# A hybrid decoder step on one core: splitting the weights with two DMAs and a negated copy, instead of a cast and a subtraction

## The chip, the core and the metric

The kernel runs on one of the eight cores of a Trainium2 chip. A core has TensorE (PE, matrix products; PEld are its weight loads), VectorE (DVE), ScalarE (ACT), GpSimd (POOL) and SyncE (SP), each with its own in-order queue of instructions, an on-chip memory (SBUF) of 128 partitions, PSUM for the results of products, and 16 DMA engines that move data between HBM and SBUF. DMAs are issued by an engine's queue: in this kernel by SP and by POOL. The metric is the device time of one execution in microseconds, median of several runs; less is better.

## The reference

One inference step of one layer: 16 meta tokens and 512 prompt tokens in one group, 8 sample tokens in another, with shared weights. Cut to what matters here:

```python
def branch_inputs(x, pos, norm_gain, w_in, q_norm_gain, k_norm_gain):
    xn = rmsnorm(x, norm_gain)
    h = jnp.einsum('btd,de->bte', xn, w_in)                  # 2048 -> 8704
    q, k, v, z_a, u, z_s, g_a, g_s = jnp.split(h, IN_SPLITS, axis=-1)
    ...

def s5_branch(u, h0, ..., w_glu, b_glu):                     # diagonal state space
    ...
    y = jax.nn.gelu(y.reshape(b, t, SSM_WIDTH))
    y = y * jax.nn.sigmoid(y @ w_glu + b_glu)                # 1024 -> 1024
    return y, h[:, -1]

def merge(x, o_attn, z_a, y_ssm, z_s, g_a, g_s, w_attn_out, w_ssm_out, w_out):
    br_a = (o_attn * jax.nn.silu(z_a)) @ w_attn_out          # 1024 -> 2048
    br_s = (y_ssm * jax.nn.silu(z_s)) @ w_ssm_out            # 1024 -> 2048
    return x + (jax.nn.sigmoid(g_a) * br_a + jax.nn.sigmoid(g_s) * br_s) @ w_out   # 2048 -> 2048
```

Between them stand attention in a sliding window of 128 keys with the meta tokens as sinks, and, for the sample tokens, attention over a cache. Everything is float32.

## The kernel before

**Products.** TensorE works in a shorter float type, float32r. To come near float32, each operand is held as two float32r parts: hi, the operand rounded, and lo, the operand minus hi, rounded. A product is the sum of three: hi*hi, hi*lo and lo*hi. Tokens are the columns: 536 of them in two halves of 268, of which most products use 260. x is kept in SBUF as xh and xl from the start to the end of the first big product.

**The weight stream.** All weights lie in one array of 208 units, each [128, 8, 128] float32 (512 KB), in the order in which they are used. The class `Stream` hands them out: `get` makes units until it is `ahead` units (2) in front of the one in use. A unit is made by `tiles` (buffers raw, whi, wlo, three of each) and `piece`: SP issues the load of raw, ACT casts it to whi, DVE subtracts whi from raw into wlo. These are recorded at high priority. `mm` (the line L843 is its matmul) takes a unit and does 8 k-tiles x 3 products x 2 halves = 48 matmuls of 260 columns into a PSUM pair; there are two such pairs. The first six units are made in pieces, between the loads of x (tiles xr, ten buffers, the name that also keeps early results; their squares are xsq), while x is split into xh and xl.

**Side work.** After each unit `mm` lets `Background.step` record side work with a budget of DVE time per unit: first the state space (`ssm_prep`, then for each of 8 blocks `ssm_consts` and `ssm_block`), then attention (`Attn`: keys, values, queries, blocks of scores, softmax, turn, weigh) and, in a second lane, the sample tokens' attention over the cache (`Attn.sample`). `bg.after` holds the side work of the attention stage behind the last subtraction of the stream.

**Stages.** Up to about 60 us: loads of x, the first units, the norm. To about 640 us: the input products beside the state space. To about 1020 us: the rest of them, the gate of the state-space branch (w_glu) and part of w_ssm_out, beside attention. From there on the last products alone. The results of an input block are scaled on DVE into z (two buffers), get their tanh on ACT, and SP stores them to HBM (gD), from where they come back later.

**Order.** A scheduler sets each engine's order at build time from the recorded work and its priorities; at run time an engine works its queue in that order, and a waiting instruction holds up those behind it. POOL's queue holds before the change: MEMSETs of the state space's tiles U, d and H (lines L333, L312, L340), the loads of the sample's work (L630 to L679), the copies of the windows, and the loads zr (L1094). SP's queue holds everything else that a DMA does, the weights (L781) among it.

Of the kernel before, what the change touches and what calls it, by code (L numbers as in the profile page):

```python
# [14 lines left out]
P = 128  # L15
# [37 lines left out]
def cmul(nc, pool, out, a, br, bi, sh, tag):  # L53
    """out = a * (br + i bi); axis 1 of a and out holds (re, im); sh: the shape behind it."""
# [12 lines left out]
def ssm_prep(nc, cst, tmp, psum, dram, R, ident, a_prm, a_h0):  # L67
    """Constants of the state space: everything [128 = (group of the pair, state), 32 pairs]."""
# [16 lines left out]
    # sin and cos: th minus multiples of pi, half-odd ones for cos  # L85
# [34 lines left out]
    # F = (lam_bar - 1) / lam  # L120
# [13 lines left out]
    # rows of Fk: F1re, Fre, F1im, Fim with F1 = lam_bar * F  # L134
# [15 lines left out]
    # lam_bar ** 2 = r2 * z  # L150
# [16 lines left out]
    def powers(tab, z, cnt, tag):  # L167
        """tab[j] = z ** j, j < cnt; returns z ** 1, 2, 4, 8."""
# [29 lines left out]
    # carry: r2 * z ** 132  # L198
# [7 lines left out]
    # lam_bar * h0, imaginary part negated  # L206
# [17 lines left out]
def ssm_consts(nc, pool, psum, R, D, ub, a_bT, a_bN, a_cT, bdm):  # L224
    """What block ub of 4 pairs needs beside u: stationaries, rotation tables, decay."""
    v = nc.vector
    ps = slice(4 * ub, 4 * ub + 4)
    # stationary of bu: rows (hi|lo copies of (even, odd) x 32 inputs), columns 128 states
# [22 lines left out]
    # C, C * lam_bar, and C * B_bar  # L251
    bN = pool.tile([P, 4, 2, 32], F32, name="bN")
# [27 lines left out]
    kh = pool.tile([P, P], F32R, name="kh")  # L280
    kl = pool.tile([P, P], F32R, name="kl")
# [5 lines left out]
    # rotation tables cos and -sin of (angle of lam_bar ** 2) * j, j < 132  # L287
# [93 lines left out]
    # states out (imaginary parts are held negated)  # L381
# [26 lines left out]
def rsqrt_dve(nc, pool, out, v_, shape, tag, end="t", iters=3):  # L408
    """out = v ** -0.5 by Newton steps from the exponent's half."""
# [11 lines left out]
class Attn:  # L421
# [12 lines left out]
    def load(self, i, W, row):  # L434
        """Block i of the raw k and q rows [128 = (2 heads, 64), 2, W], its halves swapped, and its norms."""
# [16 lines left out]
    def rope(self, parts, W, g, gs):  # L452
        """The loaded rows, normed and turned."""
# [69 lines left out]
    def scores(self, kv, b):  # L523
        """Scores of 128 queries of the 4 heads of kv: 16 meta keys, and 128 of the window."""
# [98 lines left out]
    def sample(self, a_sink, a_kc, a_vc):  # L623
# [33 lines left out]
        for b in range(8):  # L657
            nc.gpsimd.dma_start(out=qD[:, b], in_=qt[8 * b:8 * b + 8])
# [666 lines left out]
```

## Time and profile before

| | us |
|---|---|
| median of 3 runs | 1363.43 (1362.49 to 1364.37) |
| span of the profiled execution | 1363.1 |
| TensorE busy | 1349.8 |
| DVE busy | 913.0 |
| ACT busy | 405.7 |
| POOL busy | 51.8 |
| span in slices: TensorE | over 90% in all slices but two |

The profile gives one execution. The span runs from its first to its last instruction. A row of a group of instructions names the line of the kernel, the engine, the operation, the tile written and those read, the count, then busy time and the mean of one in ns, then the idle time of the engine before them and what ended most of it. An arrow "<-" in a row of waits stands between who waited and whom it waited for. In stage tables each engine has busy time and, in brackets, its number of instructions.

### The profile page before, as it was taken

Reading aid. Unit: us, or ns where it says so; the run is one execution under the profiler, and the core shown is the slowest. Engines: PE = TensorE matmul, PEld = TensorE weight load, DVE = VectorE, ACT = ScalarE, POOL = GpSimd, SP = SyncE. Lnnn points to the kernel's source line nnn. Section 1 sums busy time; section 2 is a strip of 40 time slices with the busy share of each in tenths; the row PEclk is TensorE's granted clock in tenths of the full one; section 3 lists DMA queues with packets and bytes.
Section 4 is the critical chain, followed back from the end, with each engine's and each line's share of the span. In section 5 each row is a group of like instructions: output and inputs, shape, how many; then the busy total and the mean of one; then the engine's idle time right before and its main releaser. Section 6 shows DMA issues by size and latency. Waiting matters only on the chain.

```text
span 1363.1 us, 26678 instructions
## 1 busy us (share of the span) xinstructions
PE 1349.8 (99%) x10996; PEld 1287.3 (94%) x10996; DVE 913.0 (67%) x1779; ACT 405.7 (30%) x686; POOL 51.8 (4%) x122
## 2 busy tenths in 40 slices
PE   9999999999999999999979999999999999999998
PEld 8999999999998989999979999999999999999998
DVE  8887778777968687868477688687876355422221
ACT  7323221222222222222244433335423122211110
POOL 0000000000000000000400211000010000000000
PEclk9999999999999999999999999999999999999999
DMA  8436253535353435343784346336666444444441
GB/s 264 140 116 216 94 173 111 172 94 172 107 160 106 157 105 160 94 134 110 188 234 128 107 151 200 125 120 215 190 208 200 139 140 140 141 137 140 135 136 45
DMA packets 91497, 201.18 MB, mean 148 GB/s; under 512 B 16060, under 2 KB 34732, under 8 KB 91344
## 3 DMA queue, kind: packets, MB, share of 16 engines
q1 hardware_dynamic: 86704, 185.59, 43.4%
q0 software_dynamic: 4672, 13.89, 3.8%
q8 instruction: 86, 1.41, 0.4%
q14 instruction: 35, 0.29, 0.1%
HBM read 171.06 MB, written 30.48 MB: 148 GB/s over the span
## 4 chain that ended last, share of the span: by engine, by line
PE 94%; DMA 3%; SPq 1%; DVE 1%; ACT 1%; issue 0%; DVEq 0%; ACTq 0%
PE mm L843 82%; PE aux L589 2%; PE aux L346 1%; DMA sw<-rawD 1%; PE aux L345 1%; DMA xr<-in_x 1%; PE mm L1188 1%; PE mm L930 1%; PE aux L396 1%; PE aux L534 1%; PE aux L389 1%; PE aux L535 1%; PE aux L1007 1%; PE mm L1125 1%; PE aux L570 1%; DMA rb<-rqD 0%
## 5 line engine op out<-in xcount | busy, mean ns | idle before, releaser
L782 ACT CAST whi<-raw 128x1024 fp32r<-128x1024 f32 (+3 forms) x220 | 219.9, 1004 | 713.9 <-PE mm L843 557.6
L843 PE MATMUL mm<-xh,whi 128*128 128x260 f32 (+1 forms) x2048 | 423.9, 287 | 0.0
L843 PE MATMUL mm<-xl,whi 128*128 128x260 f32 (+1 forms) x2048 | 416.3, 284 | 0.0
L843 PE MATMUL mm<-xh,wlo 128*128 128x260 f32 (+1 forms) x2048 | 416.0, 284 | 0.0
L783 DVE TENSOR_TENSOR wlo<-raw,whi 128x1024 fp32r<-128x1024 f32 (+3 forms) x220 | 255.0, 1163 | 116.2 <-ACT whi L782 112.1
L843 PEld LDWEIGHTS mm<-xh,whi 128*128 128x128 f32 x2048 | 317.5, 189 | 13.1 <-issue 8.5
L843 PEld LDWEIGHTS mm<-xl,whi 128*128 128x128 f32 x2048 | 318.3, 189 | 5.2 <-issue 5.2
L843 PEld LDWEIGHTS mm<-xh,wlo 128*128 128x128 f32 x2048 | 315.3, 188 | 2.8 <-issue 2.8
L843 PE MATMUL mm<-Y,whi 128*128 128x260 f32 x768 | 125.5, 284 | 0.0
L843 PEld LDWEIGHTS mm<-Y,whi 128*128 128x128 f32 x768 | 105.7, 188 | 2.3 <-issue 2.3
L843 PE MATMUL mm<-ml,whi 128*128 128x260 f32 x480 | 96.8, 283 | 0.0
L843 PE MATMUL mm<-mh,whi 128*128 128x260 f32 x480 | 96.4, 282 | 0.0
L843 PE MATMUL mm<-mh,wlo 128*128 128x260 f32 x480 | 96.4, 282 | 0.0
L843 PE MATMUL mm<-A,whi 128*128 128x260 f32 x512 | 82.2, 282 | 0.0
L843 PE MATMUL mm<-Y,wlo 128*128 128x260 f32 x384 | 77.6, 283 | 0.0
L843 PEld LDWEIGHTS mm<-mh,whi 128*128 128x128 f32 x480 | 73.9, 189 | 0.0
L843 PEld LDWEIGHTS mm<-ml,whi 128*128 128x128 f32 x480 | 73.8, 188 | 0.0
L843 PEld LDWEIGHTS mm<-mh,wlo 128*128 128x128 f32 x480 | 73.8, 188 | 0.0
L843 PEld LDWEIGHTS mm<-A,whi 128*128 128x128 f32 x512 | 70.2, 188 | 0.0
L870 DVE TENSOR_TENSOR z<-mm,R 128x520 f32<-128x520 f32 x43 | 30.0, 697 | 49.9 <-PE mm L843 48.6
L843 PEld LDWEIGHTS mm<-Y,wlo 128*128 128x128 f32 x384 | 59.2, 188 | 0.4 <-issue 0.4
L843 PE MATMUL mm<-A,wlo 128*128 128x260 f32 x256 | 51.6, 283 | 0.0
(371 smaller groups left out, 1467.2 us busy)
## 6 DMA issues: line engine op xcount, KB each, us to landing
raw<-in_w SPq DMA_DIRECT2D x202, 512.0 KB, 3.9
gD<-z SPq DMA_DIRECT2D x48, 260.0 KB, 2.2
t<-gD SPq DMA_DIRECT2D x32, 260.0 KB, 2.7
cache<-in_kc POOLq DMA_DIRECT2D x15, 288.0 KB, 3.5
cache<-in_vc POOLq DMA_DIRECT2D x15, 288.0 KB, 3.4
xr<-in_x SPq DMA_DIRECT2D x16, 268.0 KB, 6.3
t<-in_x SPq DMA_DIRECT2D x16, 260.0 KB, 3.5
f<-FD SPq DMA_DIRECT2D x64, 64.0 KB, 2.4
```

Source lines behind the costliest of these rows:

```text
L345: nc.tensor.matmul(bu[:, i, 0:272], lhsT=D["bh"][:, i, a], rhs=U[:, a], start=True, stop=False)
L346: nc.tensor.matmul(bu[:, i, 0:272], lhsT=D["bl"][:, i, a], rhs=U[0:64, a], start=False, stop=True)
L389: nc.tensor.matmul(y[32 * a:32 * a + 32, 0, 0:NE], lhsT=D["cl"][:, a, i], rhs=H[:, a, i, 0:NE], start=(i == 0), stop=False, skip_group_che ...
L396: nc.tensor.matmul(y[32 * a:32 * a + 32, 1, 0:272], lhsT=D["c"][:, a, i], rhs=H[:, a, i, 1:273], start=(i == 0), stop=(i == 1))
L534: nc.tensor.matmul(ps[:, e, 0:272], lhsT=q, rhs=KH[:, k0:k0 + 272], start=True, stop=False)
L535: nc.tensor.matmul(ps[:, e, 0:272], lhsT=q, rhs=KL[:, k0:k0 + 272], start=False, stop=True)
L570: nc.tensor.transpose(out=ps[:, 0, 128 * r:128 * r + 128], in_=Pn[:, r], identity=C["idn"])
L589: nc.tensor.matmul(pv[64 * e:64 * e + 64, 0, 0:256], lhsT=V[0:n, 64 * kv:64 * kv + 64], rhs=pr[:, e::2], start=(i == 0), stop=(i == len(pa ...
L782: nc.scalar.copy(out=hi, in_=raw)
L783: self.dve = nc.vector.tensor_tensor(out=lo, in0=raw, in1=hi.bitcast(F32), op=ALU.subtract).ins
L843: m = nc.tensor.matmul(ps[:, c, 0:W], lhsT=wt[:, k], rhs=xo(kt, c), start=f, stop=l)
L870: v.tensor_tensor(out=z, in0=ps, in1=R_[:, :, 8:CH], op=ALU.mult)
```

## The change

`Stream.make` takes the old way only for units below 10 (`by_dma`). From unit 10 on a unit is made by three instructions: POOL issues a DMA that loads the unit from HBM into whi and rounds it to float32r on the way; ACT copies whi, times -1, into wlo; POOL issues a second DMA that loads the unit again and adds it to what stands in wlo. whi and wlo get four buffers instead of three, and the stream runs three units ahead instead of two. raw moves to the pool of the start-up phase and is gone after it; xr has eight buffers instead of ten, xsq, bN, kh and kl one instead of two. All other DMAs that POOL issued are issued by SP. The side work is no longer held behind a subtraction of the stream.

```diff
-NXR = 10
+NXR = 8
...
     def __init__(self, tc, nc, pool, w, ahead=2):
-        self.made, self.i, self.parts = 0, 0, {}
+        self.made, self.i, self.parts, self.by_dma = 0, 0, {}, 10
 
     def tiles(self, i, pool=None):
-        raw = self.pool.tile([P, 8, P], F32, name="raw", bufs=3)
-        hi = (pool or self.pool).tile([P, 8, P], F32R, name="whi", bufs=3)
-        lo = (pool or self.pool).tile([P, 8, P], F32R, name="wlo", bufs=3)
+        raw = self.early.tile([P, 8, P], F32, name="raw", bufs=3)
+        own = 4 if pool is None else 3
+        hi = (pool or self.pool).tile([P, 8, P], F32R, name="whi", bufs=own)
+        lo = (pool or self.pool).tile([P, 8, P], F32R, name="wlo", bufs=own)
...
     def make(self, i):
         with self.tc.high_priority(offset=HIGH):
-            self.piece(i, self.tiles(i), slice(0, 8))
+            if i < self.by_dma:
+                self.piece(i, self.tiles(i), slice(0, 8))
+                return
+            nc = self.nc
+            hi = self.pool.tile([P, 8, P], F32R, name="whi", bufs=4)
+            lo = self.pool.tile([P, 8, P], F32R, name="wlo", bufs=4)
+            self.parts[i] = (hi, lo)
+
+            nc.gpsimd.dma_start(out=hi, in_=self.w[i])
+            nc.scalar.activation(out=lo, in_=hi.bitcast(F32), func=AF.Copy, scale=-1.0)
+            nc.gpsimd.dma_start(out=lo, in_=self.w[i], accum_op=ALU.add)
...
-    ws = Stream(tc, nc, wp, A["w"])
+    ws = Stream(tc, nc, wp, A["w"], ahead=3)
...
-            bg.after = (ws.dve,) if at is not None else ()
+            bg.after = ()
...
+        ws.early = xld
...
-            sq = acc if kt == 0 else xld.tile([P, 2, CH], F32, name="xsq")
+            sq = acc if kt == 0 else xld.tile([P, 2, CH], F32, name="xsq", bufs=1)
...
-            self.after = nc.gpsimd.dma_start(out=t[:, 0:n], in_=src[:, c * CK:c * CK + n]).ins
+            self.after = nc.sync.dma_start(out=t[:, 0:n], in_=src[:, c * CK:c * CK + n]).ins
...
-            nc.gpsimd.dma_start(out=zr, in_=gD[24 + b])
+            nc.sync.dma_start(out=zr, in_=gD[24 + b])
```

How the queues change is seen in the order of the built programs. A name ends in the number of its buffer; behind it stand the shape and, in brackets, the semaphores that the instruction waits for: those of an engine (PE, Activation, DVE) or of a DMA lane (DMAHW for SP's, DMASW for POOL's).

POOL before, in the second and third block of the state space: nothing but MEMSETs.

```order
L333 MEMSET U_2649 32x4x8 [waits DMAHW5_49,DMAHW4_49,DMAHW6_49,DMAHW3_49,DMAHW7_49,DMAHW2_49,PE_49]
L333 MEMSET U_2649 32x4x8 [waits Pool_49]
L312 MEMSET d0_2637 128x8 [waits DVE_49,Activation_49,Pool_49]
L340 MEMSET H_2718 128x8 [waits DVE_49,PE_49]
L333 MEMSET U_3417 32x4x8 [waits DMAHW3_49,DMAHW2_49,DMAHW6_49,DMAHW1_49,DMAHW7_49,DMAHW0_49,PE_49]
```

POOL now, at the same place (units 24 to 28; whi_1947 and wlo_1948 are one unit, whi_2019 and wlo_2020 the next):

```order
L796 DMA whi_1947<-in_w 128x1024 [waits DMASW4_49,PE_49]
L798 DMA wlo_1948<-in_w 128x1024 [waits DMASW6_49,DMASW5_49,Activation_49]
L796 DMA whi_2019<-in_w 128x1024 [waits PE_49]
L798 DMA wlo_2020<-in_w 128x1024 [waits DMASW7_49,DMASW0_49,Activation_49]
L796 DMA whi_2098<-in_w 128x1024 [waits PE_49]
L333 MEMSET U_2632 32x4x8 [waits DMAHW4_49,DMAHW3_49,DMAHW5_49,DMAHW2_49,DMAHW6_49,DMAHW1_49,PE_49]
L333 MEMSET U_2632 32x4x8 [waits Pool_49]
L798 DMA wlo_2099<-in_w 128x1024 [waits DMASW1_49,Activation_49]
L796 DMA whi_2166<-in_w 128x1024 [waits DMASW2_49,PE_49]
```

A unit's two loads now stand in turn, and the MEMSETs stand between them. The load of the next whi comes behind a load of wlo that waits for ACT.

POOL now, in the last stage: three units make a group.

```order
L796 DMA whi_15144<-in_w 128x1024 [waits DMASW2_49,PE_49]
L796 DMA whi_15197<-in_w 128x1024 [waits DMASW4_49,DMASW3_49,PE_49]
L798 DMA wlo_15145<-in_w 128x1024 [waits Activation_49]
L798 DMA wlo_15198<-in_w 128x1024 [waits DMASW6_49,DMASW5_49,Activation_49]
L796 DMA whi_15256<-in_w 128x1024 [waits PE_49]
L798 DMA wlo_15257<-in_w 128x1024 [waits DMASW7_49,Activation_49]
```

Here two loads of whi are issued before the first of the two waits for ACT; before the change POOL had nothing there.

SP now, in attention, where the sample's work has moved to it (before, the loads of the cache stood in POOL's queue):

```order
L675 DMA cache_9408<-in_kc 128x576 [waits DVE_49]
L675 DMA cache_9492<-in_kc 128x576 [waits DVE_49]
L675 DMA cache_9581<-in_kc 128x576 [waits DMAHW1_49,DVE_49]
L675 DMA cache_9665<-in_kc 128x576 [waits DMAHW2_49,DVE_49]
L675 DMA cache_9885<-in_kc 128x576 [waits DMAHW3_49,DVE_49]
L888 DMA gD_73<-z_9496 128x520 [waits DMAHW4_49,Activation_49]
```

Five loads of the cache, each waiting for DVE to be done with a buffer, now stand ahead of a store of z.

More of the change, by code (lines that the diff above doesn't have):

```diff
@@ L250, in ssm_consts @@
     yield 1.1
-    bN = pool.tile([P, 4, 2, 32], F32, name="bN")
+    bN = pool.tile([P, 4, 2, 32], F32, name="bN", bufs=1)
     nc.sync.dma_start(out=bN, in_=a_bN[:, ps])
@@ L678, in load @@
                 for r in range(4):
-                    nc.gpsimd.dma_start(out=t[r::4, n], in_=new)
+                    nc.sync.dma_start(out=t[r::4, n], in_=new)
             return t
```

22 lines of the change are left out of this document (11 added, 11 removed).

## The prediction

> **What bounds the kernel now.** I read the page first (busy times and the chain), then who waits for whom on TensorE, then the busy times by stage, and last the tiles of the weight stream.
>
> ```profile
> span 1363.1 us, 26678 instructions
> PE 1349.8 (99%) x10996; PEld 1287.3 (94%) x10996; DVE 913.0 (67%) x1779; ACT 405.7 (30%) x686; POOL 51.8 (4%) x122
> PE 94%; DMA 3%; SPq 1%; DVE 1%; ACT 1%; issue 0%; DVEq 0%; ACTq 0%
> ```
>
> TensorE is busy for 1349.8 of 1363.1 us, and 94% of the chain that ends last is TensorE itself. At most 13.3 us of the span is time in which it does nothing, whatever the other engines are spared. Who made it wait is the next view:
>
> ```profile
> engine line waited for: us in total, times, longest us
> PE aux L502 <- DVE vb L498: 4.9, 1, 4.9
> PE aux L534 <- DVE QT L519: 2.4, 2, 1.8
> ...
> PE mm L930 <- ACT whi L782: 0.6, 2, 0.3
> ```
>
> Two waits of the attention side work make 7.3 us; the weights themselves (whi) cost 0.6 us in the whole run. So the split that the change replaces is hidden now. In the page's groups it looks costly:
>
> ```profile
> L782 ACT CAST whi<-raw 128x1024 fp32r<-128x1024 f32 (+3 forms) x220 | 219.9, 1004 | 713.9 <-PE mm L843 557.6
> L783 DVE TENSOR_TENSOR wlo<-raw,whi 128x1024 fp32r<-128x1024 f32 (+3 forms) x220 | 255.0, 1163 | 116.2 <-ACT whi L782 112.1
> ```
>
> ACT mostly waits for TensorE to give a whi buffer back (557.6 us): the supply is ahead of the demand. How fast the demand is, by stage, comes from the stage table of the tile raw, which has one DVE subtraction per unit:
>
> ```profile
> 60.00:640.00 580.00, 105.03 (x88) 91.38 (x87) 1.00 0.43 136
> 640.00:930.00 290.00, 49.45 (x41) 42.04 (x40) 0.99 0.53 158
> 930.00:1020.00 90.00, 16.38 (x14) 14.08 (x14) 1.00 0.66 205
> 1020.00:1348.00 328.00, 69.75 (x57) 59.63 (x57) 1.00 0.45 140
> ```
>
> The columns are the stage, its length, DVE's and ACT's busy time (count), then the clock, the DMA engines' busy share and GB/s. TensorE takes a unit every 580/88 = 6.59 us, 290/41 = 7.07, 90/14 = 6.43 and 328/57 = 5.75 us. These are the periods that a new supply has to keep.
>
> **The change, part by part.** Of the 208 units, 198 (10 to 207) get their parts in the new way.
>
> Removed: 198 subtractions on DVE, 198 x 1.19 = 236 us (105.03/88 = 1.19 by the rows above), on an engine that is 67% busy and off the chain. Worth nothing but what the 7.3 us of attention waits hold. The cast on ACT is replaced by a scaled copy of the same size; the nearest row is the cast itself (91.38/87 = 1.05 us), so ACT's sum stays.
>
> Added: two DMAs per unit on POOL's queue, which had none of the weights. POOL works its queue in order, and the order of the built program for units 10 to 134 is nearly always: rounding load of unit i, adding load of unit i, rounding load of i+1. The adding load waits for ACT's copy, and that copy waits for the rounding load to land. So while POOL stands at the adding load, the next unit's rounding load is queued behind it. This makes one unit's supply a serial chain. Its pieces:
>
> ```profile
> L675 POOL DMA_DIRECT2D cache<-in_kc x16: 539/539/558, 668.6 to 850.0; - x16
> L781 SPq DMA_DIRECT2D raw<-in_w x87: 322/333/430, 60.1 to 635.7; - x87
> ...
> DMA to landing us min/median/max: 3.1/3.8/6.2
> 110.00:115.00 5.00, 5.00 (x44) 5.00 (x43) 3.42 (x3) 0.49 (x1) 0.00 (x0) 1.00 0.98 322
> ```
>
> The first row is POOL's own time to issue a 128-row load (min/median/max in ns): 0.54 us. The second and third are SP's loads of whole units in 60:640: 3.8 us from issue to landing. The last is a stretch in which the DMA engines were full: share 0.98 at 322 GB/s, so the 16 engines together do 329 GB/s, and a 512 KB unit occupies them for 1.6 us.
>
> What the trace does not show is an adding load. It reads a unit from HBM, reads the negated copy in SBUF, and writes the sum. Let a be its time on the DMA engines in units of a plain load's 1.6 us. The lower end is a = 1 (a load by the row above, with the second read beside it); the upper one is a = 2 (the two reads one after the other, each at that row's rate). I take a = 1.5: three streams of bytes where the row's load has two. That the rounding load takes longer than a plain one isn't shown either; below 0 is excluded, since it moves the same bytes, and I take 0 by the row of raw.
>
> Chain of a unit where the queue alternates: the adding load of i is issued (0.54), the next rounding load is issued right behind it in the same queue, so its bytes come after those of the adding load (1.6a - 0.54 later than alone), it lands after 3.8, and ACT copies for 1.05. Together 0.54 + 1.6a - 0.54 + 3.8 + 1.05 = 4.85 + 1.6a: 6.45 us for a = 1, 7.25 for 1.5, 8.05 for 2. Against the demand this gives, for a = 1.5: in 60:640 (7.25 - 6.59) x 88 = 58 us, in 640:930 (7.25 - 7.07) x 41 = 7 us. The three units that the stream is ahead hide bursts, not a mean that is too slow.
>
> From unit 135 on (930 us to the end) the built order is two rounding loads, their two adding loads, then one and one. Three units then take two such chains: 3.8 + 1.6a + 1.05 for the first; 1.6 until the second of the pair has landed; then 3.8 + 1.05 for the single one, behind what is left of two adding loads (3.2a - 1.6). That is 9.7 + 4.8a: 16.9 us at a = 1.5, or 5.63 per unit, under 6.43 and 5.75. Nothing is lost there.
>
> Costed at nothing, with the cover named. At the start, ten buffers of xr are cut to eight, and xsq has one instead of two:
>
> ```profile
> xr<-in_x SPq DMA_DIRECT2D x16, 268.0 KB, 6.3
> ```
>
> A load of x takes 6.3 us to land. With eight buffers, two of them still held for the squares, some five blocks are loaded ahead; 18 matmuls of 5.00/44 = 0.114 us (the stretch 110:115) use up a block in 2.05 us, so five are 10.3 us of cover; if that fails, two blocks fewer are worth about 4.1 us. The fourth buffer of whi and wlo is needed for the longer chain, no time by itself. POOL's MEMSETs for U, d and H now stand between weight loads:
>
> ```profile
> POOL d L312 <- ACT d L311: 106.9, 8, 16.0
> ...
> POOL cache L675 <- DVE o_p L701: 66.0, 6, 29.0
> ```
>
> Before, POOL came to them early and waited idle; now it comes to them late, behind loads that wait for TensorE themselves. I take 0, up to a wait of 16.0 us in a bad block. The loads of the sample's side work and the cache go from POOL to SP, past gD's stores and the q and k rows. A cache load that waits for DVE (up to 29.0 us, longest) now holds back the store of a z tile, of which there are two, and so the next eviction. I take 0, because DVE is spared 1.2 us per unit there; if that is wrong, up to some 20 us.
>
> In 655:675 the engines are full already:
>
> ```profile
> 655.00:675.00 20.00, 20.00 (x168) 20.00 (x168) 8.59 (x11) 3.90 (x6) 11.81 (x19) 1.00 0.98 211
> 690.00:695.00 5.00, 5.00 (x36) 4.96 (x35) 4.01 (x9) 2.45 (x7) 0.00 (x0) 0.79 0.55 151
> ```
>
> Three units' adding loads (3 x 1.6 x 1.5 = 7 us) don't fit there; of that the lead of three units hides all in a supply that keeps up, and none in one that doesn't. It is inside the 65 us below, which that stretch already has in its stage's term.
>
> **Sum**: the profiled execution's span of 1363.1 us (the median of the runs is 1363.4, so nothing lies around it) + 58 + 7 = **1428 us**.
>
> **Rivals.**
>
> The adding load costs a = 2 (or the issue or the rounding is as much slower). Then 60:640 loses (8.05 - 6.59) x 88 = 128, 640:930 (8.05 - 7.07) x 41 = 40, the last stage (9.7 + 9.6)/3 = 6.43 against 5.75, so 57 x 0.68 = 39, and 930:1020 is short of DMA: its share 0.66 of 6.43 us is 4.24, and 3.2 more is 7.44, so 14 x 1.0 = 14. Sum 221, so 1584 us. For it: an engine that has to take in twice the bytes for one write. Against: nothing in this trace. The Trainium skill, Collectives: The Full Stack, section "The bandwidth ceiling: the fold count and why AG ≠ RS ≠ AR", says that an add in the DMA path is slow not for the sum but because it needs two source reads through one read ring, and measured 62.28 against 32.35 GB/s. By that rule a would be 1.9, near this rival; no run here shows it yet.
>
> The cover holds (a near 1, chain 6.45 us under 6.59): TensorE sees no difference, 1363 us. For it: margin on paper in every stage. Against: 0.14 us of margin in the longest one.
>
> Faster: the cover holds, and DVE, without its subtractions, brings vb and QT in time. This takes away 4.9 + 2.4 us, and the slow clock after the gap (0.79 for 5 us, row above: 1.05 us), so 1355 us. It decides from a = 1.1 down, the point at which 4.85 + 1.6a is 6.59. Against: those two wait behind loads in the stretch that is full, and the change puts more there.
>
> It doesn't do what it says (the load doesn't round, and lo is nothing): the same bytes and instructions go, so no time is changed by it, and it gets no chance of its own.
>
> The Trainium skill, SBUF — State Buffer, section "Who interferes with whom", has a rule against any load from POOL's queue: DVE in its two-port modes locks GpSimd out while descriptors are written. The trace speaks against a price here: the issues of cache took 539 to 558 ns beside a DVE that is 67% busy over the run, so 0.02 us at most where the rule would allow a whole DVE operation for each issue.
>
> **How the numbers follow.** The forecast (a of about 1.2 to 1.8, 1385 to 1510 us) gets 0.40; a of 1.8 and more 0.28, 0.10 of it above 1600; a slow-down of a few us up to 1385 by the queues of POOL and SP 0.07; no difference 0.11; faster 0.14. The range, 1355 to 1600 us, leaves out 0.10 above and about 0.05 below. Faster by over 0.2% (2.7 us, about what a measurement of this kernel can tell): 0.14; within: 0.11; slower: 0.75.
>
> **What would show it.** Right: TensorE waits of some us per unit in 60:640 for wlo's adding load, TensorE busy well under 99% there, POOL waiting for ACT's copy and next to never for TensorE; few waits after 1020. Each step: issues on POOL near 0.54 us; the rounding load landing after 5 to 6 us, not 3.8; the adding load's share of the DMA engines 1.5 times that of the rounding one. Wrong: POOL waits for TensorE's buffers throughout (then the chain is shorter than I say), or the DMA share is near 1 in all stages (then bytes, not the queue, are the bound), or the lost time sits at SP's stores of z.

## The result, and the profile after

The changed kernel takes 1644.8 us (median of 4 runs, 1642.4 to 1657.6) against 1363.9 us for the kernel before on the same chip: a ratio of 1.208 (95% interval 1.204 to 1.212). That is 281 us more. The forecast was 1428 us, 65 us more, with a range that ended at 1600 us: the direction came as forecast, and so did the mechanism in the first stage; the size did not. In the runs below without adding and with the queue turned, one execution each (1432.7 and 1457.1 us) counts as disturbed: it is in the median and left out of the ratio.

The page of the changed kernel, first the sums, then the chain that ended last:

```profile
span 1655.8 us, 26713 instructions
PE 1434.6 (87%) x10996; PEld 1351.8 (82%) x10996; DVE 690.3 (42%) x1581; ACT 401.8 (24%) x686; POOL 287.7 (17%) x434
...
issue 26%; DMA 22%; PE 8%; POOL 5%; DVE 4%; ACT 2%; SPq 1%; POOLq 0%; ACTq 0%; DVEq 0%
DMA whi<-in_w 13%; PE mm L854 6%; POOL whi L796 3%; POOL wlo L798 2%; ACT wlo L797 2%; DMA cache<-in_vc 1%; DMA wlo<-in_w 1%; DMA Y<-yD 1%; DMA zr<-gD 1%; DMA sw<-rawD 1%; PE mm L1200 1%; DMA sb<-rawD 1%; DMA rb<-rqD 1%; DMA rb<-rkD 1%; DVE o_p L701 1%
```

TensorE was 94% of the chain and is now 8%. The profile follows this chain back only to about 512 us, so its shares make 68% of the span, and for 26% (issue) it shows no cause. What it names in TensorE's place is above all the rounding load of whi (13%), POOL's two issues and ACT's copy: the supply of a unit. TensorE is busy 85 us longer with as many matmuls, because the granted clock fell to a mean of 0.94 (1349.8 / 0.94 = 1436).

The view of who waits for whom, over all engines:

```profile
POOL wlo L798 <- ACT wlo L797: 1080.8, 172, 15.9
ACT wlo L797 <- DMA whi<-in_w: 661.7, 119, 10.9
...
PE mm L854 <- DMA wlo<-in_w: 107.7, 50, 6.0
...
POOL whi L796 <- PE mm L854: 51.2, 21, 11.2
```

POOL stands 1080.8 us at the adding load, waiting for ACT's copy; ACT waits for whi to land; POOL waits only 51.2 us for TensorE to give a buffer back. Before the change the supply waited for TensorE, now TensorE waits for the supply.

Where the time went is read from stretches in which the two kernels did the same matmuls. First the four stages of the kernel before, then the stretches of the changed one with as many matmuls (PE's count in brackets):

```profile
60.00:640.00 580.00, 580.00 (x4719) 543.27 (x4719) 454.33 (x964) 146.62 (x183) 3.77 (x32) 1.00 0.43 136
640.00:930.00 290.00, 282.66 (x2276) 263.73 (x2275) 205.68 (x379) 111.59 (x279) 35.26 (x62) 0.99 0.53 158
930.00:1020.00 90.00, 90.00 (x733) 84.78 (x732) 73.56 (x125) 36.03 (x78) 8.10 (x15) 1.00 0.66 205
1020.00:1348.00 328.00, 328.00 (x2736) 328.00 (x2735) 128.48 (x147) 75.04 (x85) 4.37 (x8) 1.00 0.45 140
```

```profile
57.60:760.10 702.50, 615.86 (x4719) 570.13 (x4718) 359.84 (x870) 144.22 (x184) 126.98 (x204) 0.95 0.73 174
760.10:1139.80 379.70, 310.89 (x2290) 286.05 (x2289) 179.73 (x368) 110.03 (x277) 59.20 (x84) 0.90 0.77 190
1139.80:1248.00 108.20, 93.66 (x725) 88.16 (x726) 40.26 (x79) 37.64 (x79) 18.23 (x26) 0.94 0.76 198
1248.00:1641.90 393.90, 347.66 (x2739) 342.09 (x2739) 60.65 (x90) 74.20 (x85) 80.88 (x113) 0.96 0.78 196
```

The columns behind the length are busy times of PE, PEld, DVE, ACT and POOL, then the granted clock, the DMA engines' share and GB/s. The four stages lose 702.5 - 580 = 122.5 us, 89.7, 18.2 and 65.9 us, 296 us together; that is more than the 281 of the medians because the profiled execution was the longest of the four (1657.6 us). The forecast had 58, 7, 0 and 0. The start lost nothing: the first stage begins 2.4 us earlier than before. The DMA share is 0.73 to 0.78, not 1. A unit's mean time in the first stage is 702.5 / 88 = 7.98 us.

How one unit is made is seen in the timeline from 305 us on, POOL first, then ACT's negated copies (start, length, what; in brackets the idle time before it and what ended it):

```profile
305.80 0.89 POOL L796 DMA_DIRECT2D whi<-in_w  x1
313.94 0.86 POOL L798 DMA_DIRECT2D wlo<-in_w  x1 [7.24 <-ACT wlo L797]
314.48 0.89 POOL L796 DMA_DIRECT2D whi<-in_w  x1
```

```profile
312.58 1.06 ACT L797 ACTIVATE wlo<-whi 128x1024 fp32r<-128x1024 f32 x1 [7.43 <-PE mm L854]
```

The profile puts ACT's wait down to TensorE, but the load that POOL issued at 305.80 landed after 6.7 us, at 312.5, and that is when the copy starts. From one rounding load to the next: 6.78 us until ACT can copy, 1.06 for the copy, 0.30 until POOL goes on, 0.54 between the starts of the adding load and of the next rounding load, 8.68 us in all, against a demand of 6.59. The forecast had 7.25.

### The profile page after: what moved, and what is told of

Read it like the earlier page. It is cut to its first block, busy times and chain, and to the rows that moved or that the text cites. A ratio compares the mean times of both kernels' runs of the same rounds, so it can differ in the third digit from the quotient of the medians.

```text
span 1655.8 us, 26713 instructions
## 1 busy us (share of the span) xinstructions
PE 1434.6 (87%) x10996; PEld 1351.8 (82%) x10996; DVE 690.3 (42%) x1581; ACT 401.8 (24%) x686; POOL 287.7 (17%) x434
## 3 DMA queue, kind: packets, MB, share of 16 engines
q0 software_dynamic: 57024, 207.64, 54.8%
## 4 chain that ended last, share of the span: by engine, by line
issue 26%; DMA 22%; PE 8%; POOL 5%; DVE 4%; ACT 2%; SPq 1%; POOLq 0%; ACTq 0%; DVEq 0%
DMA whi<-in_w 13%; PE mm L854 6%; POOL whi L796 3%; POOL wlo L798 2%; ACT wlo L797 2%; DMA cache<-in_vc 1%; DMA wlo<-in_w 1%; DMA Y<-yD 1%; DMA zr<-gD 1%; DMA sw<-rawD 1%; PE mm L1200 1%; DMA sb<-rawD 1%; DMA rb<-rqD 1%; DMA rb<-rkD 1%; DVE o_p L701 1%
## 5 line engine op out<-in xcount | busy, mean ns | idle before, releaser
L854 PE MATMUL mm<-xh,wlo 128*128 128x260 f32 (+1 forms) x2048 | 437.4, 296 | 70.5 <-DMA wlo<-in_w 69.8
L797 ACT ACTIVATE wlo<-whi 128x1024 fp32r<-128x1024 f32 x198 | 209.6, 1059 | 1022.2 <-DMA whi<-in_w 661.7
L854 PE MATMUL mm<-xh,whi 128*128 128x260 f32 (+1 forms) x2048 | 439.4, 297 | 4.0 <-DVE z L881 3.7
L854 PE MATMUL mm<-xl,whi 128*128 128x260 f32 (+1 forms) x2048 | 432.0, 293 | 0.0
L854 PEld LDWEIGHTS mm<-xh,wlo 128*128 128x128 f32 x2048 | 332.8, 198 | 81.3 <-DMA wlo<-in_w 77.7
L798 POOL DMA_DIRECT2D wlo<-in_w x198 | 172.3, 870 | 1232.6 <-ACT wlo L797 1080.8
L854 PEld LDWEIGHTS mm<-xh,whi 128*128 128x128 f32 x2048 | 333.7, 199 | 18.4 <-issue 9.9
L854 PEld LDWEIGHTS mm<-xl,whi 128*128 128x128 f32 x2048 | 333.9, 198 | 6.0 <-issue 5.9
L796 POOL DMA_DIRECT2D whi<-in_w x198 | 155.2, 831 | 107.0 <-PE mm L854 51.2
L1189 DVE SCALAR_TENSOR_TENSOR z<-mm,t 128x520 f32<-128x520 f32 x15 | 10.5, 699 | 181.7 <-PE mm L854 181.7
```

The costliest lines, as they stand in the source:

```text
L796: nc.gpsimd.dma_start(out=hi, in_=self.w[i])
L797: nc.scalar.activation(out=lo, in_=hi.bitcast(F32), func=AF.Copy, scale=-1.0)
L798: nc.gpsimd.dma_start(out=lo, in_=self.w[i], accum_op=ALU.add)
L854: m = nc.tensor.matmul(ps[:, c, 0:W], lhsT=wt[:, k], rhs=xo(kt, c), start=f, stop=l)
L1189: v.scalar_tensor_tensor(out=y, in0=ps, scalar=1.0 / 16, in1=xr, op0=ALU.mult, op1=ALU.add)
```

## The experiments

The theories. QUEUE: the in-order queue makes each unit a serial chain. BYTES: the adding load's time on the DMA engines. REST: the moved side loads, smaller buffers and the background's order. Each experiment is an edit of the changed kernel, unless another is named.

**Loads by themselves.** The kernel holds nothing but loads of single units and small reads by DVE that end each kind.

```diff
+        def rnd(t, i):
+            then(lambda: nc.gpsimd.dma_start(out=t.bitcast(F32R), in_=w[i]))
+        def add(t, i):
+            then(lambda: nc.gpsimd.dma_start(out=t, in_=w[i], accum_op=ALU.add))
```

> Computes none of the outputs: loads of one weight unit (512 KB) alone, four of a kind, each one when the one before has landed, then eight of a kind back to back; kinds in order: SP plain, POOL plain, POOL rounding, POOL adding to f32, POOL adding to f32r; then eight pairs each of rounding and plain, rounding and adding, SP plain and POOL adding. If the adding load is the dear one (a near 2): alone all but the adding ones land in 3.1 to 3.8 us, the adding ones in 5 to 5.5; back to back 1.6 us a unit for the first three kinds, 3.0 to 3.2 for the adding ones; pairs of rounding and adding 4.6. If the rounding load is dear: 5 us or more alone and 2.3 or more back to back, and the adding one like it. If an issue on POOL limits: all POOL kinds alike at 0.54 us or more above SP's.

POOL's issues in that run: eight plain loads (L833), then a single and eight rounding ones (L836), then a single and eight adding ones (L839):

```profile
52.63 4.16 POOL L833 DMA_DIRECT2D a<-in_w  x8 [3.64 <-DVE s L827]
...
75.77 0.53 POOL L836 DMA_DIRECT2D a<-in_w  x1 [3.66 <-DVE s L827]
...
84.54 4.22 POOL L836 DMA_DIRECT2D a<-in_w  x8 [4.13 <-DVE s L827]
...
116.83 0.85 POOL L839 DMA_DIRECT2D a<-in_w  x1 [4.90 <-DVE s L827]
122.55 7.06 POOL L839 DMA_DIRECT2D a<-in_w  x8 [4.87 <-DVE s L827]
```

DVE's reads, each of which starts when the load, or the last of the eight, is there:

```profile
65.55 1.47 DVE L827 COPY s<-a 128x1 f32<-128x1 f32 x8 [13.22 <-DMA a<-in_w]
...
79.43 0.15 DVE L827 COPY s<-a 128x1 f32<-128x1 f32 x1 [3.96 <-DMA a<-in_w]
...
97.41 1.47 DVE L827 COPY s<-a 128x1 f32<-128x1 f32 x8 [13.17 <-DMA a<-in_w]
...
122.10 0.15 DVE L827 COPY s<-a 128x1 f32<-128x1 f32 x1 [5.57 <-DMA a<-in_w]
145.57 1.47 DVE L827 COPY s<-a 128x1 f32<-128x1 f32 x8 [23.31 <-DMA a<-in_w]
```

This run is a single execution. Alone, a rounding load takes 79.43 - 75.77 = 3.7 us from its issue to DVE's read, an adding one 122.10 - 116.83 = 5.3 us. Eight plain loads take 12.92 us, eight rounding ones 12.87, eight adding ones 23.02. With the single one taken off, the other seven need 1.31 us each for the rounding kind and 2.53 us for the adding kind: 1.93 times as much. That was expected as 3.0 to 3.2 us against 1.6: both are shorter, and the ratio holds. Rounding costs nothing here; adding nearly doubles. The Trainium skill, Collectives: The Full Stack, section "The bandwidth ceiling: the fold count and why AG ≠ RS ≠ AR", gave 62.28 / 32.35 = 1.93 for an add in the DMA path of a collective; this run agrees with the ratio.

**No adding.** The second load overwrites the copy instead of being added to it.

```diff
-            nc.gpsimd.dma_start(out=lo, in_=self.w[i], accum_op=ALU.add)
+            nc.gpsimd.dma_start(out=lo, in_=self.w[i])
```

> The second load overwrites the negated copy instead of adding to it (lo is then w and not the remainder; the products are as many). Order and waits stay. If the adding load's longer stay on the DMA engines made the chain longer than forecast (a near 2 instead of 1): the rounding load behind it lands about 1.5 us earlier than 7.1 us, the chain is about 7.2 us instead of 8.7, and with (7.2 - 6.59) x 88 + (7.2 - 7.07) x 41 = 59 us lost, the time is about 1425 to 1460 us. If the rounding load is slow by itself, or the queue's issue is, whatever is queued ahead of it: the landing stays at 7 us and the time at 1600 us or more. If the chain had nothing to do with it (REST): 1645 us.

1415.9 us (1.034, 1.026 to 1.042; single executions from 1399.8 to 1432.7): 229 us of the 281 are gone with the order untouched, somewhat more than the 1425 to 1460 us that were expected. Here the chain is that of a = 1. By equal matmul counts the first stage loses 7.5 us, the second 39.3, the third 1.6 and the last 1.0. What the load behind it feels shows in the page's rows on landing, first of the changed kernel, then of this one:

```profile
whi<-in_w POOLq DMA_DIRECT2D x198, 512.0 KB, 7.1
```

```profile
whi<-in_w POOLq DMA_DIRECT2D x198, 512.0 KB, 5.2
```

The rounding load itself is the same in both and lands 1.9 us earlier behind a plain load.

**The queue turned.** POOL has the rounding load of unit i+1 ahead of the adding load of unit i.

```diff
-            nc.gpsimd.dma_start(out=hi, in_=self.w[i])
-            nc.scalar.activation(out=lo, in_=hi.bitcast(F32), func=AF.Copy, scale=-1.0)
-            nc.gpsimd.dma_start(out=lo, in_=self.w[i], accum_op=ALU.add)
+            m = nc.gpsimd.dma_start(out=hi, in_=self.w[i])
+            self.open.append((i, hi, lo))
+            if len(self.open) > 1:
+                with self.tc.issue_after(m.ins):
+                    self.finish()
...
+    def finish(self):
+        nc = self.nc
+        i, hi, lo = self.open.pop(0)
+        nc.scalar.activation(out=lo, in_=hi.bitcast(F32), func=AF.Copy, scale=-1.0)
+        nc.gpsimd.dma_start(out=lo, in_=self.w[i], accum_op=ALU.add)
...
```

> The same instructions as the change, but POOL's queue holds the rounding load of unit i+1 ahead of the adding load of unit i. Theory QUEUE (the loss is the chain of one unit, 8.7 us in 300:340 of the changed kernel, because the next rounding load stands behind an adding load that waits): two units share one chain, 4.35 us a unit, under every stage's demand (5.75 to 7.07 us): about 1370 us, 1360 to 1400, and the whi loads then wait for TensorE's buffers. Theory BYTES (the two loads of a unit occupy the DMA engines for 4.58 us, 54.8% of 1655.8 us for 198 units, and all other queues for 321 us; the engines don't get past the share of 0.8 that the stages show): (198 x 4.58 + 321) / 0.8 = 1535 us or more, the landing of whi longer than 7.1 us. Theory REST (the moved side loads and the smaller buffers cost the time): no change from 1645 us.

1448.6 us (1.059, 1.053 to 1.065): the same instructions and bytes as the change, 196 us faster. Who waits for whom, and the last stage by equal matmul counts (columns as above):

```profile
POOL whi L797 <- PE mm L867: 865.9, 182, 46.4
...
POOL wlo L807 <- ACT wlo L806: 192.9, 87, 15.2
```

```profile
1103.80:1432.70 328.90, 327.99 (x2734) 327.77 (x2733) 61.58 (x90) 73.76 (x80) 79.70 (x112) 1.00 0.98 233
```

POOL is back to waiting for TensorE. The last stage takes 328.9 us, against 328.0 before and 393.9 with the change, although the DMA engines are at 0.98. So it was the order, and not the bytes, that cost 66 us there. QUEUE alone gave 1370 us, and that is missed: 17 us stay in the first stage, 58 and 11 us in the two with attention beside the weights. BYTES alone, 1535 us or more, is further off. Loading whi from SP's queue, which would take it out from behind the adding loads altogether, was not measured.

**Both at once, and the rest alone.** Turned queue with the overwriting load; then everything of the change but its split, on three buffers of raw, whi and wlo; then no second load at all.

```diff
-        nc.gpsimd.dma_start(out=lo, in_=self.w[i], accum_op=ALU.add)
+        nc.gpsimd.dma_start(out=lo, in_=self.w[i])
```

> The turned queue and the overwriting second load in one kernel (lo is w and not the remainder). Each of the two alone took 1645 us down by 196 and 229 us and left 85 and 53 over the kernel before. If what each left is the other's cause (the engines full at a = 2; the chain at a = 1): both gone, 1363 to 1375 us. If what they left is the attention stage's side work in its new place (DVE stands at cache loads there, up to 12.5 us at a time, in the turned run): about 1400 to 1425 us, with PE's waits in 700 to 1050 alone.

```diff
-            nc.gpsimd.dma_start(out=hi, in_=self.w[i])
-            nc.scalar.activation(out=lo, in_=hi.bitcast(F32), func=AF.Copy, scale=-1.0)
-            nc.gpsimd.dma_start(out=lo, in_=self.w[i], accum_op=ALU.add)
+            nc.sync.dma_start(out=raw, in_=self.w[i])
+            nc.scalar.copy(out=hi, in_=raw)
+            nc.vector.tensor_tensor(out=lo, in0=raw, in1=hi.bitcast(F32), op=ALU.subtract)
...
```

> All of the change but the split: the units from 10 on are loaded by SP, cast by ACT and subtracted by DVE as before, with three buffers each and two units ahead; the moved side loads, the smaller start-up buffers and the background without its wait for the subtraction stay. As forecast (these edits cost nothing): 1363 us within 0.3%. If they are what keeps 75 us of the attention stage (700 to 1050) in the run with the turned queue: about 1400 to 1440 us. If the background without its wait is worth the attention waits of before: 1355 us.

```diff
-            nc.gpsimd.dma_start(out=lo, in_=self.w[i], accum_op=ALU.add)
```

> No second load at all: wlo is the negated copy of whi alone (the remainder is left out of the sum). POOL's queue has only the rounding loads, 1.25 us of the DMA engines for a unit. If the rounding load by itself costs nothing: the weights keep up everywhere, DMA share under 0.5, and the time is that of the rest of the change: 1363 us, or 1400 us and more if the side work is what holds the attention stage. If the rounding load is slow in the kernel: waits for whi and 1400 us and more, spread over 60 to 640 too.

They take 1390.5 us (1.019, 1.018 to 1.021), 1386.0 us (1.016, 1.015 to 1.018) and 1386.0 us (1.016, 1.015 to 1.018). All three lie between the times that were expected, near 1363 and from 1400 on. The table sets the medians of the four combinations beside each other:

| us | second load overwrites | second load adds |
|---|---|---|
| turned order | 1390.5 | 1448.6 |
| the change's order | 1415.9 | 1644.8 |

Adding alone costs 58 us, the order alone 25 us, both together 254 us. They don't add, because a unit's chain costs time only by what it exceeds the demand: 8.68 us is over 6.59, and either remedy takes it near or under that.

Without a second load the rounding load lands in 3.7 us, as SP's plain loads did (3.8):

```profile
whi<-in_w POOLq DMA_DIRECT2D x198, 512.0 KB, 3.7
```

And some 21 us remain when the weights are cheap. In the run without a second load they all lie in the second stage (columns as above), which takes 311.1 us against 290; the first and last stages are within 2 us of before.

```profile
639.50:950.60 311.10, 291.82 (x2279) 270.56 (x2278) 181.05 (x369) 112.11 (x278) 21.94 (x42) 0.96 0.56 162
```

In the run with the split of before, about 7.5 us lie in the first 60 us and 16 us between 640 and 1020 us. The first of these is this experiment's own, since the changed kernel starts earlier than before, not later.

**Where the 21 us are from.** Five runs undo one part each. On the run with the split of before: the side loads back on POOL; the background's wait back.

```diff
-            self.after = nc.sync.dma_start(out=t[:, 0:n], in_=src[:, c * CK:c * CK + n]).ins
+            self.after = nc.gpsimd.dma_start(out=t[:, 0:n], in_=src[:, c * CK:c * CK + n]).ins
...
```

> As the run with the split of before and the rest of the change (1386 us), but the side loads of the sample, the cache, zr and the window stand on POOL's queue again, as in the kernel before. If their move to SP costs the 16 us that this run loses between 640 and 1020: about 1370 us (the 7 us of the start stay). If the background without its wait for the subtraction costs them: 1386 us.

```diff
...
-            bg.after = ()
+            bg.after = (ws.dve,) if at is not None else ()
```

> As the run with the split of before and the rest of the change (1386 us), but each piece of the background waits for the last subtraction in the order again, as in the kernel before; the side loads stay on SP. If the background's order costs the 16 us: about 1370 us. If the move of the side loads does: 1386 us.

1378.2 us (1.012, 1.010 to 1.013) and 1370.2 us (1.006, 1.005 to 1.007): they took away 8 and 16 us. With the split of before the missing wait alone accounts for the 16 us, so the side loads' 8 us can't be added to it. The same two on the run without a second load, where the wait is for the negated copy, then both of them, and last the buffers of bN, kh and kl:

```diff
-            nc.scalar.activation(out=lo, in_=hi.bitcast(F32), func=AF.Copy, scale=-1.0)
+            self.dve = nc.scalar.activation(out=lo, in_=hi.bitcast(F32), func=AF.Copy, scale=-1.0).ins
...
-            bg.after = ()
+            bg.after = (ws.dve,) if at is not None else ()
```

> The run without the second load (1386 us; the remainder is left out of the sum), with each piece of the background waiting for the last negated copy in the order. With the split of before the same wait took 16 us off. If the wait sets the order in which the attention's pieces stand, whatever makes the weights: about 1366 to 1370 us. If it was worth something only as a brake on DVE's subtractions and the background among them: 1386 us, as in the turned run, where it gave nothing.

```diff
-            self.after = nc.sync.dma_start(out=t[:, 0:n], in_=src[:, c * CK:c * CK + n]).ins
+            self.after = nc.gpsimd.dma_start(out=t[:, 0:n], in_=src[:, c * CK:c * CK + n]).ins
...
```

> The run without the second load (1386 us; the remainder is left out of the sum), with the side loads of the sample, the cache, zr and the window on POOL's queue again, behind the rounding loads. If the move to SP is what costs the 21 us between 640 and 930 (the chain there runs through SP's q rows and z stores): about 1365 to 1370 us. If POOL's queue holds them up behind weight loads that wait for TensorE: 1386 us or more. If neither queue matters and the order of DVE's side work does: 1386 us.

> The run without the second load (1386 us; the remainder is left out of the sum), with both the side loads on POOL's queue and the background's wait (for the last negated copy) as before. Each alone gave nothing (1385 us and 1385 us). If the two cover for each other, so that either one left wrong costs the whole: about 1365 to 1370 us. If the 21 us come from what DVE and ACT now do in another order, the subtractions being gone, or from the single buffers of bN, kh and kl: 1385 us.

```diff
-    bN = pool.tile([P, 4, 2, 32], F32, name="bN", bufs=1)
+    bN = pool.tile([P, 4, 2, 32], F32, name="bN")
...
```

> The run without the second load (1386 us; the remainder is left out of the sum), with two buffers each for bN, kh and kl again, as before. If their single buffers hold back the state space's constants, and with them the stage up to 930: about 1365 to 1370 us. If not: 1385 us.

1385.1, 1384.7, 1382.4 and 1387.5 us: nothing beyond 4 us. So the 21 us of the kernel with cheap weights aren't the side loads' queue, the wait, or these buffers. Their cause stays open. One candidate is that DVE's and ACT's work stands in another order when the subtractions are gone; that wasn't tested. The waits of TensorE in the run without a second load, the first two of them here, point to the attention's pieces, of which vb was waited for as long in the kernel before:

```profile
PE aux L570 <- DVE Pm L562: 5.1, 1, 5.1
PE aux L502 <- DVE vb L498: 4.9, 1, 4.9
...
```

The wait was also tried in the turned run:

```diff
-            bg.after = ()
+            bg.after = (ws.dve,) if at is not None else ()
...
-        nc.scalar.activation(out=lo, in_=hi.bitcast(F32), func=AF.Copy, scale=-1.0)
+        self.dve = nc.scalar.activation(out=lo, in_=hi.bitcast(F32), func=AF.Copy, scale=-1.0).ins
```

> The turned queue, with each piece of the background waiting for the last negated copy in the order, as it waited for the subtraction before. If the two losses add: 1449 us less the 16 us that the wait was worth with the split of before, about 1430 us; no more, since 59 us of the turned run are the adding load's time on full DMA engines. If the wait has nothing to hold on to here: 1449 us.

1450.0 us (1.066, 1.060 to 1.071), as without it.

**Two plain loads for an adding one, and the strict order.** In the first, a second plain load into a spare buffer stands behind an overwriting one; the second is the change itself. In both, POOL's order is held strictly to one unit after the other.

```diff
-            nc.gpsimd.dma_start(out=hi, in_=self.w[i])
+            with ExitStack() as st:
+                if self.prev is not None:
+                    st.enter_context(self.tc.issue_after(self.prev))
+                nc.gpsimd.dma_start(out=hi, in_=self.w[i])
...
-            nc.gpsimd.dma_start(out=lo, in_=self.w[i], accum_op=ALU.add)
+            m = nc.gpsimd.dma_start(out=lo, in_=self.w[i])
+            x = self.pool.tile([P, 8, P], F32, name="wx", bufs=1)
+            with self.tc.issue_after(m.ins):
+                self.prev = nc.gpsimd.dma_start(out=x, in_=self.w[i]).ins
```

> In place of the adding load two plain ones: one into wlo (over the negated copy), one into a buffer that nobody reads; the order is rounding load, plain load, plain load, next rounding load (lo is w and not the remainder). If the adding load holds the chain up by the DMA engines' time alone (2.50 us back to back, two plain loads of 1.26): as the change, about 1645 us, 1600 to 1680. If it is its longer issue on POOL (0.87 instead of 0.54 us) or another trait of adding that no plain load has: nearer to the run with one plain load, 1416 to 1500 us.

1911.6 us (1.401, 1.398 to 1.404), far over what either theory gave. The strict order was a second edit that the expectation had not priced: the change's own order has two rounding loads in a row here and there, and these share one chain. So the change itself was run in the strict order, with its adding load as it is:

```diff
+            with ExitStack() as st:
+                if self.prev is not None:
+                    st.enter_context(self.tc.issue_after(self.prev))
+                nc.gpsimd.dma_start(out=hi, in_=self.w[i])
...
+            self.prev = nc.gpsimd.dma_start(out=lo, in_=self.w[i], accum_op=ALU.add).ins
```

> The change with POOL's order made strict: rounding load, adding load, rounding load of the next unit, in every unit, also where the change's order has two rounding loads ahead of two adding loads. It is the like of the run with two plain loads (1912 us), which was strict too. If the adding load is two plain loads to the DMA engines: 1912 us less the third issue of a unit (198 x 0.52 = 103 us), about 1810 us; from the chain of 8.7 us that single units take in 300:340 of the changed kernel, (8.7 - 6.59) x 88 + (8.7 - 7.07) x 41 + (8.7 - 6.43) x 14 + (8.7 - 5.75) x 57 and 20 us of the rest, about 1835 us. If the order's pairs are worth nothing: 1645 us, and two plain loads are then dearer than an adding one.

1827.1 us (1.339, 1.333 to 1.345). The pairs are worth 182 us to the change. The run with two plain loads is 4.6% longer (1912 us); if its third issue of a unit is counted in full (103 us), 1930 us stand beside the 1912. So to the chain an adding load is about two plain ones. POOL's timeline of the strict run, then ACT's copy:

```profile
305.90 0.87 POOL L800 DMA_DIRECT2D whi<-in_w  x1
313.56 0.87 POOL L802 DMA_DIRECT2D wlo<-in_w  x1 [6.79 <-ACT wlo L801]
314.11 0.89 POOL L800 DMA_DIRECT2D whi<-in_w  x1
```

```profile
312.20 1.06 ACT L801 ACTIVATE wlo<-whi 128x1024 fp32r<-128x1024 f32 x1 [1.79 <-DMA whi<-in_w]
```

A unit takes 314.11 - 305.90 = 8.21 us here. The formula 4.85 + 1.6a gives 8.05 for a = 2, and the step from ACT's end at 313.26 to POOL's start at 313.56, which it left out, is 0.30 us more.

No version beats the kernel before: the best one that makes its weights in the new way and computes the same is the turned queue, 1448.6 us.

## Why the prediction was right in kind and wrong in size

**What bounds the kernel** held: TensorE was the bound, the split was hidden, and no run without those 236 us of DVE work was faster than before. DVE's busy time fell from 913 to 690 us while the time rose by 281.

**The serial chain on POOL's queue** was the mechanism in the place forecast, the first stage: POOL waits for ACT's copy and little for TensorE; of the 86.6 us in which TensorE is idle there, 64.7 are waits for the adding load; the DMA share stays under 0.8. The turned queue shows it: the same work in another order is 196 us faster. That few waits would come behind 1020 us was wrong: TensorE waits 37.9 us for the adding load in the last stage.

**The price of the adding load** is the step that failed first. The prediction took a = 1.5 of a plain load's 1.6 us, 2.4 us. By itself an adding load keeps the engines for 2.53 us, 1.93 plain loads of 1.31; that is hardly more than 2.4. In the kernel, with other traffic beside it, both are longer. A rounding load lands after 3.7 us with nothing ahead of it. In the two strict runs it lands after 6.5 us behind an adding load, and after 6.1 us behind two plain ones:

```profile
whi<-in_w POOLq DMA_DIRECT2D x198, 512.0 KB, 6.5
```

```profile
whi<-in_w POOLq DMA_DIRECT2D x198, 512.0 KB, 6.1
```

The adding load is issued 0.54 us ahead, so it delays the load behind it by 6.5 - 3.7 + 0.54 = 3.3 us, which is a = 2.1 in the prediction's unit. The first of the two plain ones is issued 1.05 us ahead, so they make 3.45 us, 1.7 each. The ratio is again 1.9. So the rival with a = 2 had the right term, and the forecast was 0.9 us a unit short, most of it by the ratio and some 0.2 us by the plain load's own size. The argument for 1.5, three streams of bytes against two, doesn't fit the loads alone; two reads, one after the other, do fit, but no run tells why. By the time of its packets alone the adding load is 1.7 plain ones: both kinds take 54.8% of 1655.8 us, 907 us, where two plain ones take 47.5% of 1411.9, 671 us.

**The first stage.** The chain of a single unit was 8.2 to 8.7 us instead of 7.25: 0.9 us by the adding load, 0.3 by the hand-over from ACT to POOL, which had no term. Against this stood something else left out: "nearly always" hid the places where two rounding loads stand in a row. The strict run's first stage takes 761.2 us, 181 more than before, the change's 122.5 more. So it is luck that the rival's 128 us for this stage is near the truth: it left out the hand-over, which adds time, and the pairs, which save some.

**The second stage** is the largest miss: 90 us instead of 7, and 40 with 8.05 us a unit. Here the forecast had the wrong path. TensorE is idle for 379.7 - 310.9 = 68.8 us, and next to none of that is put down to the weights; it waits for pieces of the attention, for which the sum had no term:

```profile
PE aux L570 <- DVE S L540: 18.3, 4, 8.1
PE aux L502 <- issue: 14.7, 1, 14.7
...
PE mm L854 <- DMA wlo<-in_w: 5.2, 2, 2.6
```

One of these waits shows how a late load reaches TensorE through ACT's queue:

```profile
1040.58 1.06 ACT L797 ACTIVATE wlo<-whi 128x1024 fp32r<-128x1024 f32 x1 [7.27 <-DMA whi<-in_w]
1041.55 0.68 ACT L538 COPY S<-aux 128x288 f32<-128x288 f32 x2
```

```profile
1041.96 0.78 DVE L540 COPY_PREDICATED S<-k_mprev,aux 128x256 f32<-128x256 int32 x2 [15.01 <-ACT S L538]
```

```profile
1042.45 1.12 PE L570 MATMUL aux<-k_idn,Pn 128*128 128x128 f32 x4 [5.16 <-DVE S L540]
```

The scores that ACT copies into S were done at 1034.4, but the copy stands in ACT's queue behind the negated copy, which waits for whi until 1040.58. Not every wait is of this kind: the longest, 14.7 us at L502, ends with DVE's vb, which waited for a side load of sb that SP issued at 816.94 and that took 12.0 us to land. How the 90 us divide is open: in this stage the turned queue still loses 58 us, the run without adding 39, and the one without a second load 21.

**The third stage** lost 18 us instead of none. TensorE's waits there, 8.4 us for Y and 5.5 for S, aren't for the weights either.

**The last stage** was to lose nothing and lost 66 us. Its cycle of three units was put at 9.7 + 4.8a, 16.9 us. POOL's timeline there shows one:

```profile
1401.11 1.44 POOL L796 DMA_DIRECT2D whi<-in_w  x2
1409.44 0.89 POOL L798 DMA_DIRECT2D wlo<-in_w  x1 [6.90 <-ACT wlo L797]
1410.92 0.86 POOL L798 DMA_DIRECT2D wlo<-in_w  x1 [0.59 <-ACT wlo L797]
1411.47 0.88 POOL L796 DMA_DIRECT2D whi<-in_w  x1
1422.82 0.86 POOL L798 DMA_DIRECT2D wlo<-in_w  x1 [10.48 <-ACT wlo L797]
1423.36 1.45 POOL L796 DMA_DIRECT2D whi<-in_w  x2
```

22.25 us from pair to pair; over the stage the mean is 3 x 393.9 / 57 = 20.7, where the demand is 17.3. The single rounding load, behind two adding loads, is what was too cheap: from its issue at 1411.47 to the adding load at 1422.82 are 11.35 us, of which 1.06 and 0.30 are the copy and the hand-over, so 10.0 us for the load, where the step had 3.8 + 3.2a - 1.6 = 7.0 (8.6 for a = 2). That is 3.0 of the 5.35 us by which the cycle is longer than forecast.

**Costed at nothing.** The start, its buffers and the MEMSETs cost nothing: the first stage starts 2.4 us early, and the kernel without a second load is within 2 us of before in it. The side loads on SP were put at 0 with a bound of 20 us, and the background's order had no term: with the split of before they cost 16 us, and 21 us of unproved cause stay with the weights on POOL. "DVE is spared" was no cover for them.

**The cover.** At a = 1 it held in the first stage nearly as the second rival said: 7.5 us lost in the run without adding, for a formula that gave 6.45 us against 6.59.

**The issue on POOL.** The Trainium skill, SBUF — State Buffer, section "Who interferes with whom", lets DVE lock POOL out while descriptors are written. No price of it is seen: an adding load's issue took 0.85 us in the run of loads alone, where DVE hardly works, and 0.86 in the timelines of the changed kernel; whether DVE was in such a mode at these moments is not shown.

**The clock.** The prediction had no term for it. TensorE's gaps came with a granted clock of 0.90 to 0.96 in the four stages, and 85 us of added busy time. Where the supply sets the pace a slower matmul fills time that would be idle, so this isn't 85 us of the 281; how much of it counts was not measured.

**The range** ended at 1600 us because the rival with a = 2 gave 1584. What the rival left out, the attention's waits, the hand-over and the single load of the last stage, made the time longer and outweighed the pairs.

## What to carry to other kernels

A queue that works in order turns "load, wait for another engine, load again" into a serial chain: write down what stands in front of the next item's first load, and put that load ahead of the waiting one. The same goes for the engine that waits for the load: what stands behind its wait is late too. Compare the whole chain with the demand of each stage, hand-overs included; only the excess costs time, so two remedies may each seem to be worth nearly the whole loss. Count an adding DMA as two loads, and don't lengthen the supply of the bound engine to spare one that is hidden.

## What was not expected of the hardware

The DMA engines moved more than the full stretch of the kernel before (322 GB/s at a share of 0.98) had suggested. In the run of loads alone, the slices of the span show it:

```profile
GB/s 70 89 135 396 161 134 141 277 286 130 101 216 398 72 70 84 108 205 211 97 96 111 75 144 211 209 168 413 410 138 185 270 282 277 113 211 273 276 274 130
```

Plain and rounding loads reach 396 to 413 GB/s, adding ones 205 to 211, with a unit's bytes counted once. The 1.6 us of the prediction, from 329 GB/s, was therefore too long for a plain load alone (1.31 us), and a little short for one in the kernel (1.7 us).

An adding load takes longer to issue too: 0.85 us against 0.53 in the rows above. In the kernel POOL starts its next load 0.54 us after it, but the issue of that load then takes 0.89 us, and 0.53 in the run without adding: it ends some 0.35 us later. How much of the 3.3 us above is this wasn't separated.
